# Feed-forward activations transposed by 32x32 blocks and transfers within SBUF in place of TensorE

## The chip, the cores and the metric

The kernel runs on one core of a Trainium2 chip. A core has five engines with instruction streams of their own: TensorE (PE in the profile, its weight loads PEld), VectorE (DVE), ScalarE (ACT), GpSimd (POOL) and SyncE (SP), which only issues transfers. Sixteen DMA engines carry the transfers. Working memory is SBUF with 128 partitions; matrix products land in PSUM. The metric is device time of one execution in microseconds.

## The reference

One layer of a diffusion backbone: modulated norm, a joint input projection, two kinds of attention, an output projection, and a SwiGLU feed-forward block. All is float32. What matters here is the last block, with 256 tokens, `D_MODEL` 2048 and `D_FF` 5632:

```python
def swiglu_sublayer(x, shift, scale, gate, norm_g, w_ff_gate, w_ff_up, w_ff_down):
    h = modulate(rms_norm(x, norm_g), shift, scale)
    return x + gate * ((jax.nn.silu(h @ w_ff_gate) * (h @ w_ff_up)) @ w_ff_down)
```

`gate` (called `a5` in the kernel) is one of six rows of `silu(c) @ w_ada + b_ada`.

## The kernel before

Every float32 operand of a product is split in two float32r parts, `hi` (rounded) and `lo` (the rest), and each product is three matmuls: hi x hi, hi x lo, lo x hi (`mm3`, lines 212 to 214).

`project` computes 256 tokens by 512 columns. It walks the contraction in steps of two 128-row tiles. For each step `load_w` brings 128x2x512 weights (512 KB) by one transfer on SP's queue into one of seven buffers `wraw` (line 200); ScalarE casts them to `whi` (L207), VectorE subtracts to `wlo` (L208), both in three buffers each; TensorE then does twelve matmuls of 512 columns, six for each of the two tiles of 128 tokens (`tk`).

The feed-forward block is a loop of eleven column groups `cg` of 512. In each, a gate product of eight steps ends in `g_evac` (ScalarE's Silu into `act`, L941) and an up product of eight steps ends in `u_evac` (VectorE multiplies, L944). The result `act[tk]` holds tokens on partitions and columns along the free dimension; the down product needs columns on partitions. So `turn` lets TensorE transpose four 128x128 pieces into PSUM (`ftp`, L951), and `split` writes `hi` and `lo` of the transposed tile `fT` (ScalarE L217, VectorE L218). `after(n, f)` puts `f` off by `n` steps, counting from the step in which it is called, so that the engines have other work meanwhile: `turn` runs in the first and second step of the next product. The down product (four groups of 22 steps, weights `w_ff_down`) comes behind the loop.

From `cg` 2 on, two more loads of 512 KB stand behind each product: pieces of `w_ada` (`wada`, line 388), which take `wraw` buffers too, and which VectorE adds up into `a5` (L395).

The framework's scheduler sets the order of each engine's instructions when the program is built, and puts in the semaphore waits. Each engine takes its own instructions strictly in order. Transfers issued by SP use eight semaphores in turn (DMAHW0 to DMAHW7), and each transfer waits until the last one of its own semaphore has landed: at most eight of SP's transfers are in flight. A weight load waits besides for the subtraction that frees its buffer.

Of the kernel before, what the change touches and what calls it, by code (L numbers as in the profile page):

```python
# [17 lines left out]
P = 128  # L18
# [27 lines left out]
def hybrid_block(ctx: ExitStack, tc: tile.TileContext, t: dict, out: bass.AP):  # L46
    nc = tc.nc
# [9 lines left out]
    def big_tile(name, dt=F32):  # L57
        return big.tile([P, 2048], dt, tag="big", name=name)
# [4 lines left out]
    def tp_ps(name="tp"):  # L63
        return psum.tile([P, CG], F32, tag="tp", bufs=2, name=name)
# [4 lines left out]
    def scratch(name, n=CG, dt=F32, tag="scr", bufs=3):  # L69
        return scr.tile([P, n], dt, tag=tag, bufs=bufs, name=name)  # L70
# [5 lines left out]
    ident = tab.tile([P, P], F32, name="ident")  # L76
# [139 lines left out]
    def split(hi, lo, src):  # L216
        nc.scalar.copy(out=hi, in_=src)  # L217
        nc.vector.tensor_tensor(out=lo, in0=src, in1=hi.bitcast(F32), op=ALU.subtract)  # L218
# [165 lines left out]
    def ada_pieces(a, chunk):  # L384

        for kt, hf in [(kt, hf) for kt in range(NKT) for hf in range(2)]:
            wt = wp.tile([P, 1024], F32, tag="wraw", bufs=WRAW, name="wada2")
            nc.sync.dma_start(out=wt, in_=w_ada[kt * P:(kt + 1) * P, chunk * D + hf * 1024: chunk * D + (hf + 1) * 1024])
            dst = a[:, hf * 1024:(hf + 1) * 1024]
            yield None  # L390
            with tc.issue_after(last_lo[-1].ins):
                if kt == 0:
                    nc.vector.tensor_scalar(out=dst, in0=wt, scalar1=sc[:, 0, 0:1], scalar2=None, op0=ALU.mult)
                else:
                    nc.vector.scalar_tensor_tensor(out=dst, in0=wt, scalar=sc[:, 0, kt:kt + 1], in1=dst, op0=ALU.mult, op1=ALU.add)  # L395
# [94 lines left out]
    def take(gen, n):  # L490
        for _ in range(n):
            if next(gen, gen) is gen:
                return

    def drain(gen):
        for _ in gen:
            pass
# [9 lines left out]
    def after(n, fn):  # L507
        late.append([n, fn])
# [66 lines left out]
    def project(src, hl, nkt, c0, evac, kt0=0, side=None, head=1, tail=1, hook=None):  # L575


        ps = [mm_ps() for _ in range(2)]
        nt = nkt // WK
        order = [(i, tk) for i in range(nt) for tk in range(2)]  # L580
        order[:2 * head] = [(i, tk) for tk in range(2) for i in range(head)]
        order[-2 * tail:] = [(i, tk) for tk in range(2) for i in range(nt - tail, nt)]
        wt = {}
        for n, (i, tk) in enumerate(order):
            if i not in wt:
                wt[i] = load_w(src, i * WK * P, c0, in_big=WHI <= i < head or nt - tail <= i < nt - WHI)
            wh, wl = wt[i]
            for j in range(WK):
                k = i * WK + j
                ah, al = hl.at(kt0 + k, tk * P, P)  # L590
                mm3(ps[tk], ah, al, wh[:, j], wl[:, j], k == 0, k == nkt - 1)
            if i == nt - 1 and (tail > 1 or tk == 1):
                for x in ([tk] if tail > 1 else range(2)):
                    evac(x, ps[x])
            if hook:
                hook(i, tk)
            if n % 2:
                tick()
                if side:
                    side()  # L600
                yield None
# [24 lines left out]
    def q_evac(qT, br):  # L626
        def f(tk, ps):
            o = norm_rope(ps, br, "q", tk)

            def turn():  # L630
                tp = tp_ps("qtp")
                for h in range(4):
                    nc.tensor.transpose(out=tp[:, h * P:(h + 1) * P], in_=o[:, h * P:(h + 1) * P], identity=ident)
                src = tp.rearrange("p (h q) -> p h q", h=4)
                split(qT[:, 0, :, tk * P:(tk + 1) * P], qT[:, 1, :, tk * P:(tk + 1) * P], src)
            after(5 + tk, turn)
        return f
# [79 lines left out]
    def unit(br, u):  # L717
        return (u // 4, u % 4) if br == "a" else (u // 8, u // 2 % 4)
# [59 lines left out]
    for n, (br, u) in enumerate(units):  # L778
        q = (br, unit(br, u)[0])
# [33 lines left out]
    for cg in range(4):  # L813
# [19 lines left out]
        def gated(tk, ps):  # L833
            g = gs[tk]
            nc.vector.tensor_tensor(out=g, in0=ps, in1=g, op=ALU.mult)
            nc.vector.tensor_tensor(out=m[tk], in0=m[tk], in1=g, op=ALU.add)
            after(2 + tk, turn(tk))

        def turn(tk, cg=cg, m=m):
            def f():  # L840
                tp = tp_ps("mtp")
                for j in range(4):
                    nc.tensor.transpose(out=tp[:, j * P:(j + 1) * P], in_=m[tk][:, j * P:(j + 1) * P], identity=ident)
                hi, lo = mT.four(cg, tk * P, P)
                split(hi, lo, tp.rearrange("p (h q) -> p h q", h=4))
            return f
# [84 lines left out]
    w_g, w_u, w_d = t["w_ff_gate"][0], t["w_ff_up"][0], t["w_ff_down"][0]  # L931
    NFT = DFF // P
    fT = Parts("fT", NFT)
    for cg in range(DFF // CG):
        if cg == 2:
            a5 = big_tile("ada5")
            a5_gen = ada_pieces(a5, 5)
        act = [scratch(f"act{tk}") for tk in range(2)]

        def g_evac(tk, ps):  # L940
            nc.scalar.activation(out=act[tk], in_=ps, func=AF.Silu)  # L941

        def u_evac(tk, ps):
            nc.vector.tensor_tensor(out=act[tk], in0=ps, in1=act[tk], op=ALU.mult)  # L944
            after(2 + tk, turn(tk))

        def turn(tk, cg=cg, act=act):
            def f():
                tp = tp_ps("ftp")
                for j in range(4):  # L950
                    nc.tensor.transpose(out=tp[:, j * P:(j + 1) * P], in_=act[tk][:, j * P:(j + 1) * P], identity=ident)  # L951
                hi, lo = fT.four(cg, tk * P, P)
                split(hi, lo, tp.rearrange("p (h q) -> p h q", h=4))
            return f

        drain(project(w_g, hT, NKT, cg * CG, g_evac, **(dict(head=TURN2, hook=head_hook) if cg == 0 else {})))
        if cg > 1:
            take(a5_gen, 2)
        drain(project(w_u, hT, NKT, cg * CG, u_evac))
        if cg > 1:  # L960
            take(a5_gen, 2)
# [47 lines left out]
```

## Time and profile before

| what | us |
|---|---|
| timed runs (3), median (lowest, highest) | 1733.82 (1732.61, 1733.86) |
| span of the profiled execution | 1730.7 |
| TensorE busy in it | 1706.1 |
| VectorE / ScalarE / GpSimd busy | 1132.6 / 775.0 / 135.5 |
| first and last transpose of `ftp` | 1041.8 and 1491.2 |

The profiled execution's time from its first instruction to its last is the span; the profile gives no other time for that execution. The median of the timed runs is 3.1 us above it, for what lies around the span. In the profile a row of the timeline reads: start in us, duration, engine, line, operation, output <- input. A q behind an engine's name means its instruction queue: a row of SPq is the issue of a transfer, not the transfer. Times within the feed-forward block are given on the span's clock.

### The profile page before, as it was taken

How to read it: one execution, taken by the hardware profiler on the slowest of the kernel's cores; microseconds unless marked ns; L12 is line 12 of the kernel's file. 1: busy time of each engine (PE TensorE's matmuls, PEld its weight loads, DVE VectorE, ACT ScalarE, POOL GpSimd, SP SyncE). 2: the span in 40 equal slices, each digit the busy share in tenths (PEclk: the TensorE clock that was granted, in tenths of full speed). 3: DMA queues.
4: the chain of work that ended last, by engine and by line, in shares of the span. 5: the costliest groups of instructions: out<-in, count | busy, mean ns of one | idle time of the engine just before them, and what ended most of it. 6: DMA issues, size and time to landing. Idle time of an engine off the chain costs nothing.

```text
span 1730.7 us, 21827 instructions
## 1 busy us (share of the span) xinstructions
PE 1706.1 (99%) x8150; PEld 1378.5 (80%) x8150; DVE 1132.6 (65%) x1428; ACT 775.0 (45%) x1063; POOL 135.5 (8%) x204
## 2 busy tenths in 40 slices
PE   7999999999999999999999999999999999999998
PEld 5667778887787788888888788888888888888887
DVE  5754668888788879796665754555565665454554
ACT  5222223245656556667544444444444444333332
POOL 2100001001131120002110100000000000000000
PEclk9999999999999999999999999999999999999999
DMA  9877785687766676777796766677777777666662
GB/s 263 300 242 265 233 319 174 201 271 235 252 189 202 212 265 217 247 227 248 249 323 222 237 180 190 201 237 241 234 242 234 240 236 231 208 213 197 221 205 88
DMA packets 192010, 397.69 MB, mean 230 GB/s; under 512 B 13504, under 2 KB 25872, under 8 KB 191392
## 3 DMA queue, kind: packets, MB, share of 16 engines
q1 hardware_dynamic: 183952, 369.71, 66.2%
q0 software_dynamic: 7952, 26.58, 4.8%
q8 instruction: 64, 1.05, 0.2%
q14 instruction: 42, 0.34, 0.1%
HBM read 385.72 MB, written 10.52 MB: 229 GB/s over the span
## 4 chain that ended last, share of the span: by engine, by line
PE 88%; DVE 5%; issue 3%; DMA 1%; ACT 1%; POOL 1%; SPq 0%; DVEq 0%; ACTq 0%; POOLq 0%
PE mm L212 26%; PE mm L213 26%; PE mm L214 26%; PE ada L268 2%; DVE wlo L208 1%; PE ptp L687 1%; PE o L705 1%; DMA wraw<-in_w_in_dram 1%; PE ftp L951 1%; PE s L667 1%; ACT whi L207 1%; PE o L213 0%; PE o L214 0%; PE o L212 0%; PE s L212 0%
## 5 line engine op out<-in xcount | busy, mean ns | idle before, releaser
L208 DVE TENSOR_TENSOR wlo<-wraw,whi 128x1024 fp32r<-128x1024 f32 (+1 forms) x506 | 611.6, 1210 | 460.2 <-ACT whi L207 458.8
L207 ACT CAST whi<-wraw 128x1024 fp32r<-128x1024 f32 (+1 forms) x506 | 527.7, 1043 | 796.6 <-PE mm L214 682.0
L213 PE MATMUL mm<-wlo,hT 128*128 128x512 f32 x696 | 271.0, 389 | 2.0 <-DVE wlo L208 2.0
L212 PE MATMUL mm<-whi,hT 128*128 128x512 f32 x696 | 272.8, 392 | 0.0
L214 PE MATMUL mm<-whi,hT 128*128 128x512 f32 x696 | 271.3, 390 | 0.1
L212 PE MATMUL mm<-whi,xT 128*128 128x512 f32 x640 | 257.2, 404 | 0.6 <-ACT whi L207 0.6
L213 PE MATMUL mm<-wlo,xT 128*128 128x512 f32 x640 | 251.5, 393 | 0.9 <-DVE wlo L208 0.9
L214 PE MATMUL mm<-whi,xT 128*128 128x512 f32 x640 | 250.5, 392 | 0.0
L213 PEld LDWEIGHTS mm<-wlo,hT 128*128 128x128 f32 x696 | 130.7, 188 | 28.8 <-DVE wlo L208 2.4
L214 PEld LDWEIGHTS mm<-whi,hT 128*128 128x128 f32 x696 | 130.6, 188 | 27.9 <-DVE hT L218 0.5
L395 DVE SCALAR_TENSOR_TENSOR ada<-wada,sc,ada 128x1024 f32<-128x1024 f32 x120 | 152.0, 1277 | 0.0
L212 PEld LDWEIGHTS mm<-whi,hT 128*128 128x128 f32 x696 | 130.7, 188 | 26.3
L212 PEld LDWEIGHTS mm<-whi,xT 128*128 128x128 f32 x640 | 120.1, 188 | 37.3 <-issue 9.8
L213 PEld LDWEIGHTS mm<-wlo,xT 128*128 128x128 f32 x640 | 120.8, 189 | 25.1 <-DVE wlo L208 2.4
L214 PEld LDWEIGHTS mm<-whi,xT 128*128 128x128 f32 x640 | 120.3, 188 | 25.4
L212 PE MATMUL mm<-whi,fT 128*128 128x512 f32 x352 | 137.2, 390 | 0.0
L214 PE MATMUL mm<-whi,fT 128*128 128x512 f32 x352 | 137.0, 389 | 0.0
L213 PE MATMUL mm<-wlo,fT 128*128 128x512 f32 x352 | 136.9, 389 | 0.0
L212 PEld LDWEIGHTS mm<-whi,fT 128*128 128x128 f32 x352 | 66.1, 188 | 14.5 <-issue 0.8
L212 PE MATMUL mm<-whi,cT 128*128 128x512 f32 x192 | 75.5, 393 | 1.8 <-ACT cT L344 1.8
L214 PEld LDWEIGHTS mm<-whi,fT 128*128 128x128 f32 x352 | 66.1, 188 | 13.9
L213 PEld LDWEIGHTS mm<-wlo,fT 128*128 128x128 f32 x352 | 66.1, 188 | 13.4
(237 smaller groups left out, 2115.2 us busy)
## 6 DMA issues: line engine op xcount, KB each, us to landing
wada<-in_w_ada_dram SPq DMA_DIRECT2D x192, 512.0 KB, 4.6
wraw<-in_w_in_dram SPq DMA_DIRECT2D x154, 512.0 KB, 4.6
wraw<-in_w_ff_gate_dram SPq DMA_DIRECT2D x88, 512.0 KB, 4.5
wraw<-in_w_ff_up_dram SPq DMA_DIRECT2D x88, 512.0 KB, 3.8
wraw<-in_w_ff_down_dram SPq DMA_DIRECT2D x88, 512.0 KB, 4.8
wraw<-in_w_br_a_dram SPq DMA_DIRECT2D x32, 512.0 KB, 5.0
wraw<-in_w_out_dram SPq DMA_DIRECT2D x32, 512.0 KB, 5.1
wraw<-in_w_br_b_dram SPq DMA_DIRECT2D x16, 512.0 KB, 5.4
```

Source lines behind the costliest of these rows:

```text
L207: last_hi.append(nc.scalar.copy(out=hi[:, 0:nk], in_=raw[:, 0:nk]))
L208: last_lo.append(nc.vector.tensor_tensor(out=lo[:, 0:nk], in0=raw[:, 0:nk], in1=hi[:, 0:nk].bitcast(F32), op=ALU.subtract))
L212: nc.tensor.matmul(ps, lhsT=ah, rhs=wh, start=first, stop=False)
L213: nc.tensor.matmul(ps, lhsT=ah, rhs=wl, start=False, stop=False)
L214: return nc.tensor.matmul(ps, lhsT=al, rhs=wh, start=False, stop=last)
L268: last_pe[0] = nc.tensor.matmul(aps[32 * g:32 * g + 32, 0:ncol], lhsT=cst[:, k, :], rhs=rhs, start=(k < 4), stop=(k >= NKT - 4))
L395: nc.vector.scalar_tensor_tensor(out=dst, in0=wt, scalar=sc[:, 0, kt:kt + 1], in1=dst, op0=ALU.mult, op1=ALU.add)
L667: nc.tensor.matmul(sps[i], lhsT=qT[rows, x, hh, tk * P:(tk + 1) * P], rhs=kT["b", grp][y][rows, hh, :], start=(n == 0), stop=(n == 2))
L687: nc.tensor.transpose(out=tp[:, kt * P:(kt + 1) * P], in_=p[:, kt * P:(kt + 1) * P], identity=ident)
L705: nc.tensor.matmul(op[:, 0:BV], lhsT=pT[:, kt, :], rhs=vb[:, kt, hh * BV:(hh + 1) * BV], start=(kt == 0), stop=(kt == 3))
L951: nc.tensor.transpose(out=tp[:, j * P:(j + 1) * P], in_=act[tk][:, j * P:(j + 1) * P], identity=ident)
```

## The change

`turn` goes. In `u_evac` VectorE transposes the tile within 32x32 blocks by one instruction (`fpart`), and sixteen transfers on SP's queue move each block of 32 partitions to where the full transpose has it (`fturn`): each moves 32 partitions by four runs of 32 floats, 16 KB. Eight of a tile's transfers are put off by 8 + 2 `tk` steps, the other eight by 9 + 2 `tk`, the split by 12 + 2 `tk`. The split now reads SBUF, not PSUM. The names `fpart` and `fturn` use scratch buffers (tags `nr` and `sq`, two each) that nothing else uses in this block.

```diff
+    def turned(src, dst_hi, dst_lo, tk):
+        part = scratch("fpart", tag="nr", bufs=2)
+        nc.vector.transpose(out=part, in_=src)
+        whole = []
+        def move(part_rows):
+            if not whole:
+                whole.append(scratch("fturn", tag="sq", bufs=2))
+            sv = part.rearrange("p (k b j) -> p b k j", k=4, b=4)
+            dv = whole[0].rearrange("p (k a j) -> p a k j", k=4, a=4)
+            for a in part_rows:
+                for b in range(4):
+                    nc.sync.dma_start(out=dv[32 * b:32 * b + 32, a], in_=sv[32 * a:32 * a + 32, b])
+        after(8 + 2 * tk, lambda: move((0, 1)))
+        after(9 + 2 * tk, lambda: move((2, 3)))
+        after(12 + 2 * tk, lambda: split(dst_hi, dst_lo, whole[0].rearrange("p (k q) -> p k q", k=4)))
...
         def u_evac(tk, ps):
             nc.vector.tensor_tensor(out=act[tk], in0=ps, in1=act[tk], op=ALU.mult)
-            after(2 + tk, turn(tk))
-
-        def turn(tk, cg=cg, act=act):
-            def f():
-                tp = tp_ps("ftp")
-                for j in range(4):
-                    nc.tensor.transpose(out=tp[:, j * P:(j + 1) * P], in_=act[tk][:, j * P:(j + 1) * P], identity=ident)
-                hi, lo = fT.four(cg, tk * P, P)
-                split(hi, lo, tp.rearrange("p (h q) -> p h q", h=4))
-            return f
+            turned(act[tk], *fT.four(cg, tk * P, P), tk)
```

SP's queue from behind the up product of group 2 to behind that of group 3, before (numbers in the names of `wada` are the buffer's; xN counts equal rows in a row):

```order
L200 DMA wraw<-in_w_ff_gate_dram 128x2x512 x8
L388 DMA wada_10082<-in_w_ada_dram 128x1024
L388 DMA wada_10085<-in_w_ada_dram 128x1024
L200 DMA wraw<-in_w_ff_up_dram 128x2x512 x8
L388 DMA wada_10236<-in_w_ada_dram 128x1024
```

The same stretch of SP's queue after the change:

```order
L200 DMA wraw<-in_w_ff_gate_dram 128x2x512 x7
L947 DMA fturn<-fpart 32x4x32 x8
L200 DMA wraw<-in_w_ff_gate_dram 128x2x512
L947 DMA fturn<-fpart 32x4x32 x8
L388 DMA wada_10145<-in_w_ada_dram 128x1024
L388 DMA wada_10148<-in_w_ada_dram 128x1024
L200 DMA wraw<-in_w_ff_up_dram 128x2x512
L947 DMA fturn<-fpart 32x4x32 x8
L200 DMA wraw<-in_w_ff_up_dram 128x2x512
L947 DMA fturn<-fpart 32x4x32 x8
L200 DMA wraw<-in_w_ff_up_dram 128x2x512 x6
```

The 32 transfers of a group stand between the seventh gate load and the third up load of the next group; the first eight come one place ahead of the last gate load. Seven rows of them with the semaphores that each waits for, from the first on (the first also waits for the block transpose, on VectorE's semaphore):

```order
L947 DMA fturn<-fpart 32x4x32 [waits DMAHW5_49,DVE_49]
L947 DMA fturn<-fpart 32x4x32
L947 DMA fturn<-fpart 32x4x32 [waits DMAHW7_49]
L947 DMA fturn<-fpart 32x4x32 [waits DMAHW0_49]
L947 DMA fturn<-fpart 32x4x32 [waits DMAHW1_49]
L947 DMA fturn<-fpart 32x4x32 [waits DMAHW2_49]
L947 DMA fturn<-fpart 32x4x32 [waits DMAHW3_49]
```

Each transfer takes the next of the eight semaphores, as the weight loads do. ScalarE, from the first cast into that group's `fT` on, before:

```order
L217 CAST fT_9943<-ftp 128x4x128
L207 CAST whi<-wraw 128x1024
L217 CAST fT_9943<-ftp 128x4x128
L207 CAST whi<-wraw 128x1024 x5
L941 ACTIVATE act_9916<-mm 128x512
L941 ACTIVATE act_9917<-mm 128x512
```

and after (the two rows of `whi` shown are the casts of the first and the second up load):

```order
L217 CAST fT_9965<-fturn 128x4x128
L207 CAST whi<-wraw 128x1024
L960 ACTIVATE act_9977<-mm 128x512
L960 ACTIVATE act_9978<-mm 128x512
L207 CAST whi<-wraw 128x1024
L217 CAST fT_9965<-fturn 128x4x128
```

The casts of `fT` moved from the start of the gate product to behind it, the second between the casts of the second and the third up load; the gate evacuations moved ahead of the second up load's cast. On TensorE, the first matmuls of the third up load's step, before:

```order
L212 MATMUL mm_10087<-whi_10127,hT1_8911 128x512
L213 MATMUL mm_10087<-wlo_10128,hT1_8911 128x512
L214 MATMUL mm_10087<-whi_10127,hT1_8911 128x512
L212 MATMUL mm_10087<-whi_10127,hT1_8911 128x512
L213 MATMUL mm_10087<-wlo_10128,hT1_8911 128x512
```

and after:

```order
L212 MATMUL mm_10150<-whi_10207,hT1_8911 128x512
L212 MATMUL mm_10151<-whi_10207,hT1_8911 128x512
L213 MATMUL mm_10150<-wlo_10208,hT1_8911 128x512
L214 MATMUL mm_10150<-whi_10207,hT1_8911 128x512
L212 MATMUL mm_10150<-whi_10207,hT1_8911 128x512
```

The second tile's L212 moved ahead of the first tile's L213, the first matmul that reads `wlo`.

## The prediction

> **What bounds the kernel now.** I read the page first, then the chain of waits, then the feed-forward stage by windows.
>
> ```profile
> span 1730.7 us, 21827 instructions
> PE 1706.1 (99%) x8150; PEld 1378.5 (80%) x8150; DVE 1132.6 (65%) x1428; ACT 775.0 (45%) x1063; POOL 135.5 (8%) x204
> ...
> PE 88%; DVE 5%; issue 3%; DMA 1%; ACT 1%; POOL 1%; SPq 0%; DVEq 0%; ACTq 0%; POOLq 0%
> PE mm L212 26%; PE mm L213 26%; PE mm L214 26%; PE ada L268 2%; DVE wlo L208 1%; PE ptp L687 1%; PE o L705 1%; DMA wraw<-in_w_in_dram 1%; PE ftp L951 1%; PE s L667 1%; ACT whi L207 1%; PE o L213 0%; PE o L214 0%; PE o L212 0%; PE s L212 0%
> ```
>
> TensorE is the bound, and the transposes to be removed (L951) stand on the chain with 1%. Two windows of the gate/up stage:
>
> ```profile
> core 0: us, PE busy (x) PEld busy (x) DVE busy (x) ACT busy (x) POOL busy (x), PEclk, DMA share, GB/s
> 1180.00:1220.00 40.00, 40.00 (x179) 33.11 (x178) 24.48 (x22) 16.11 (x18) 0.00 (x0) 1.00 0.74 236
> 1340.00:1380.00 40.00, 40.00 (x182) 33.14 (x181) 24.39 (x23) 17.53 (x19) 0.00 (x0) 1.00 0.78 239
> ```
>
> TensorE never pauses there, at full clock, while VectorE has 15 of 40 us free and the DMA engines a quarter. So time taken from TensorE shortens the run, but only while weights keep arriving. The change spends exactly that: places in SP's queue.
>
> **What leaves TensorE.** The groups of the transposed tile, and the first transpose on the timeline:
>
> ```profile
> L951 PE MATMUL ftp<-ident,act x88: 270/272/273, 1041.8 to 1491.2; 128*128 128x128 f32 x88
> L217 ACT CAST fT<-ftp x22: 579/580/581, 1043.0 to 1492.0; 128x512 fp32r<-128x512 f32 x22
> L218 DVE TENSOR_TENSOR fT<-ftp,fT x22: 681/683/685, 1044.3 to 1493.3; 128x512 fp32r<-128x512 f32 x22
> ```
>
> ```profile
> 1130.31 0.39 PE L213 MATMUL mm<-wlo,hT 128*128 128x512 f32 x1
> 1130.54 0.39 PE L214 MATMUL mm<-whi,hT 128*128 128x512 f32 x1
> 1130.77 0.60 PE L951 MATMUL ftp<-ident,act 128*128 128x128 f32 x4
> 1131.12 0.47 PE L212 MATMUL mm<-whi,hT 128*128 128x512 f32 x1
> 1131.43 0.39 PE L213 MATMUL mm<-wlo,hT 128*128 128x512 f32 x1
> ```
>
> Durations overlap, so starts must be used. Product matmuls start 0.227 apart. The L213 at 1131.43 puts its predecessor's start at 1131.20; the four transposes began at 1130.77, so they cost 0.43 to 0.44 us. 22 tiles x 0.44 = **9.7 us** leave TensorE. [...]
>
> **What VectorE and ScalarE gain.** 22 block transposes of 128x512. The nearest rows are an operation of that shape and the evacuations around it:
>
> ```profile
> 1127.75 1.28 DVE L944 TENSOR_TENSOR act<-mm,act 128x512 f32<-128x512 f32 x2
> ...
> 1148.22 1.05 ACT L207 CAST whi<-wraw 128x1024 fp32r<-128x1024 f32 x1 [1.66 <-PE mm L214]
> 1150.94 0.60 ACT L941 ACTIVATE act<-mm 128x512 f32<-128x512 f32 x1 [0.76 <-PE mm L214]
> ...
> 1152.51 1.23 DVE L208 TENSOR_TENSOR wlo<-wraw,whi 128x1024 fp32r<-128x1024 f32 x1 [1.97 <-ACT whi L207]
> ```
>
> I take 0.64 us each (bounds 0.3 and 1.3: half and twice). A pair adds 1.3 us ahead of the next `wlo`; the three `whi`/`wlo` buffers put that one a step (2.7 us) ahead of its matmul, so it is hidden. Without that cover a pair would cost 1.3 us, 14 us over eleven. The transposed tile is not needed before the down product, some 20 us to 450 us later, so its own lateness costs nothing by itself; what it can delay is what stands behind its cast on ScalarE and its subtraction on VectorE. Those wait for the sixteenth landing of their tile. The two splits keep their shapes and only read SBUF: I cost them at nothing. The ScalarE order (gate evacuations now ahead of the second up cast) leaves that `wlo` about ready when needed: nothing, with no cover left.
>
> **What SP gains: the disputed cost.** 352 transfers of 16 KB join 20 loads per group. Before:
>
> ```profile
> 1127.86 0.37 SPq L200 DMA_DIRECT2D wraw<-in_w_ff_gate_dram  x1
> 1130.58 3.06 SPq L388 DMA_DIRECT2D wada<-in_w_ada_dram  x2
> 1136.49 14.43 SPq L200 DMA_DIRECT2D wraw<-in_w_ff_up_dram  x8
> ...
> 1139.68 8.20 SPq L200 DMA_DIRECT2D wraw<-in_w_ff_up_dram  x5
> ...
> 1142.40 0.37 SPq L200 DMA_DIRECT2D wraw<-in_w_ff_up_dram  x1
> ```
>
> Columns: start, duration, engine, line. These are the last gate load, two `wada`, and the first three up loads, the place where the 32 transfers go. Prices of issue and of landing:
>
> ```profile
> 1.19 0.41 SPq L88 DMA_DIRECT2D cin<-in_c_ctx_dram  x1
> 1.65 0.41 SPq L99 DMA_DIRECT2D vec<-in_b_ada_dram  x1
> 2.11 0.42 SPq L100 DMA_DIRECT2D vec<-in_norm_g_dram  x1
> ...
> 14.77 5.07 SPq L96 DMA_DIRECT2D tok<-in_ctx_dram  x8
> ```
>
> ```profile
> L200 SPq DMA_DIRECT2D wraw<-in_w_ff_up_dram x88: 367/368/401, 989.6 to 1459.1; - x88
> ...
> L388 SPq DMA_DIRECT2D wada<-in_w_ada_dram x128: 328/340/642, 152.2 to 1422.8; - x128
> ...
> DMA to landing us min/median/max: 3.5/4.4/8.4
> ```
>
> ```profile
> GB/s 263 300 242 265 233 319 174 201 271 235 252 189 202 212 265 217 247 227 248 249 323 222 237 180 190 201 237 241 234 242 234 240 236 231 208 213 197 221 205 88
> ...
> wraw<-in_w_ff_gate_dram SPq DMA_DIRECT2D x88, 512.0 KB, 4.5
> wraw<-in_w_ff_up_dram SPq DMA_DIRECT2D x88, 512.0 KB, 3.8
> ...
> cin<-in_c_dram SPq DMA_DIRECT2D x1, 8.0 KB, 1.7
> ```
>
> Unhindered SP issues start 0.46 us apart; a load of three dimensions takes 0.04 longer than one of two (368 against 328), so a transfer of this kind gets **0.50 us** (0.46 at best). The eight `tok` loads take 0.64 us each though an issue lasts 0.33: each waits for the landing of the transfer eight places earlier, because SP has eight semaphores in turn. Lone landings lie between 3.5 and 4.5 us; I take **4.0**, near the 3.8 of the up loads. Loads that queue follow each other by 512 KB at 323 GB/s = 1.62 us. A small transfer lands in about 1.7 us, hidden by the eight places.
>
> By hand, on the clock of those rows. The products by the up matmul end at 1129.03, the first block transpose at 1129.7. SP, which wanted to issue the last gate load at 1127.86, stands at the first transfer until then. Eight transfers: gate load 1133.7, landed 1137.7. Eight more: the eighth goes at 1137.7. `wada` 1138.2 and 1138.7, first up load 1139.2; they land at 1142.2, 1143.8, 1145.4. Of the next eight the sixth, seventh and eighth wait for those three landings, so the second up load goes at 1145.9 (before: 1139.68) and lands at 1149.9; the last of the next eight waits for it, and the third up load goes at 1150.4 (before: 1142.40), landing at 1154.4. The second tile's sixteenth transfer, issued at 1149.9, lands about 1151.6; its cast of 0.58 us is done on ScalarE before that load arrives, so the new wait of ScalarE is hidden behind the load, as long as the load is late. Cast 1.05 and subtraction 1.22 with hand-overs: `wlo` ready at 1156.75.
>
> When is it needed? The gate product ended at 1150.94, so the up product began at 1150.78, now 0.88 earlier for two removed transposes; its third load comes after 24 matmuls of 0.227 = 5.44, at 1155.3, and two L212 now stand ahead of the first L213: 1155.8. **TensorE waits 1.0 us** in such a group. `wada` loads stand between gate and up loads in eight groups; the other three I cost at nothing, since without the two `wada` the walk's third load goes at least 1.0 us (two issues) and up to 4.2 us (two queued loads as well) sooner, which covers the 1.0; without that cover they would cost 3 us together. GpSimd's queue gets nothing new. After the third load SP has no transfer left until the next group, some 28 us later, and six loads at 1.62 us are caught up well before. Eight x 1.0 = 8.0.
>
> **Sum.** -9.7 + 8.0 = -1.7 us on a span of 1730.7, that is 1729.0; the timed median 1733.8 lies 3.1 above that span, so **1732 us**.
>
> **Rivals.** First, the cover holds. With 0.46 us an issue and 3.5 us a landing the same walk has the third up load issued at 1148.8, landed at 1152.3 and `wlo` ready at 1154.65, 1.1 before need: all of the 9.7 us stays, 1724. For it speaks the many lone landings below 4; against it that the transfers have one dimension more than the 0.46 rows.
>
> Second, slower, by the same eight places: with landings of 4.5, the gate loads' median, four landings in a row push the third up load to 1151.9, landed 1156.4, ready 1158.75: 2.95 us a group, 23.6 in eight, +13.9, 1748. It is slower from the wait that eats the gain, 1.2 us a group, a landing of 4.1. Against it: the gate median includes loads that queue.
>
> Third, small packets fill the DMA engines. Each transfer is 128 runs of 128 bytes, eight for each of 16 engines. Two mixes of packets, the whole span and its microseconds 20 to 60:
>
> ```profile
> q1 hardware_dynamic: 183952, 369.71, 66.2%
> ```
>
> ```profile
> q1 hardware_dynamic: 10367, 9.90, 78.2%
> ```
>
> The first gives 0.662 x 1730.7 x 16 / 183952 = 100 ns for 2010 bytes, the second 48 ns for 955. So 128 bytes cost between 6 (by bytes) and 48 ns; I take 20, as the two are nearly in proportion: 0.16 us a transfer, 5 us in a 44 us group, a share of 0.75 going to 0.87. From 45 ns (11.5 us) nothing is left; at 50 ns a group runs 1.8 us over beside the 1.0 above, 8 x 2.8 - 9.7 = +13, 1747. [...]
>
> **Chances.** Wait of 0.4 to 2.2 us a group, the forecast: 0.43 (own range 1727 to 1742). Cover holds: 0.27. Landings of 4.5: 0.18. Packets: 0.08. Something on VectorE or ScalarE: 0.04, counted as slower. What a measurement can tell from no change is 0.2%, 3.5 us: 1730.3 to 1737.3. The forecast's part below that is 0.10, inside 0.22, above 0.11. Faster 0.27 + 0.10 = 0.37; same 0.22; slower 0.11 + 0.18 + 0.08 + 0.04 = 0.41. The range runs from the cover that holds, 1723.5, to landings of 4.5 and full engines, 1750; 0.04 below and some 0.12 above are left out.
>
> **What the profile after would show.** Right: no L951, 22 block transposes near 0.6 us; gaps of about 1 us on TensorE before the third up load, released by ScalarE's cast or VectorE's `wlo`, those released by a load's landing; SP rows waiting for DMAs. Cover holds: no such gaps. Packets: DMA share near 1 and landings of all loads longer. The prediction is wrong if block transposes exceed 1.3 us, if landings fall below 3.5 or pass 4.5 beside the transfers, or if the issue interval is not 0.46 to 0.50.

## The result, and the profile after

| | us, median (lowest to highest) | ratio to before, 95% interval |
|---|---|---|
| before, same chip | 1733.84 (1732.61 to 1734.24) | |
| after | 1788.49 (1784.17 to 1793.64) | 1.0318 (1.0302 to 1.0335) |

The change made the kernel 3.2% slower; 1732 was forecast. The profiled execution of after is the longest of its four, 1793.64 us with a span of 1791.9. Head and chain of its page:

```profile
span 1791.9 us, 22208 instructions
PE 1724.5 (96%) x8062; PEld 1375.7 (77%) x8062; DVE 1145.7 (64%) x1450; ACT 776.7 (43%) x1063; POOL 134.7 (8%) x204
...
PE 70%; DMA 10%; DVE 8%; issue 4%; SPq 4%; ACT 3%; POOL 1%; ACTq 0%; DVEq 0%; POOLq 0%
PE mm L213 21%; PE mm L214 21%; PE mm L212 21%; DMA wraw<-in_w_ff_up_dram 6%; DVE wlo L208 4%; SPq L947 3%; DMA wraw<-in_w_in_dram 3%; ACT whi L207 3%; PE ada L268 1%; PE ptp L687 1%; PE o L705 1%; PE s L667 1%; PE o L213 0%; PE o L212 0%; PE o L214 0%
```

TensorE's share of the chain fell from 88% to 70%. In its place stand the up loads (`wraw<-in_w_ff_up_dram`, 6%), the steps behind them (`wlo`, `whi`) and the issue of the new transfers (SPq L947, 3%). The two windows shown of before, now of after, and two rows of its waits (total, times, longest):

```profile
1180.00:1220.00 40.00, 39.24 (x168) 31.82 (x168) 22.91 (x22) 14.16 (x15) 0.00 (x0) 0.98 0.65 207
1340.00:1380.00 40.00, 36.24 (x156) 28.63 (x155) 23.41 (x23) 16.02 (x17) 0.00 (x0) 1.00 0.64 199
```

```profile
ACT whi L207 <- DMA wraw<-in_w_ff_up_dram: 86.4, 48, 5.4
...
PEld mm L212 <- ACT whi L207: 37.0, 27, 2.7
```

TensorE now pauses, ScalarE waits 86 us for up loads, and the DMA engines are less busy than before (0.65 for 0.74): they are not what is full. Where the time went by stage, from the first matmul on `hT` (gate and up) and on `fT` (down); these rows are of before, then of after:

```profile
L212 PE MATMUL mm<-whi,hT x696: 388/389/477, 989.4 to 1483.0; 128*128 128x512 f32 x174
L212 PE MATMUL mm<-whi,fT x352: 389/389/499, 1484.8 to 1724.6; 128*128 128x512 f32 x176
```

```profile
L212 PE MATMUL mm<-whi,hT x696: 387/389/628, 997.8 to 1542.2; 128*128 128x512 f32 x174
L212 PE MATMUL mm<-whi,fT x352: 387/389/632, 1542.9 to 1785.9; 128*128 128x512 f32 x176
```

The gate/up stage grew from 1484.8 - 989.4 = 495.4 us to 545.1, what follows it from 245.9 to 249.0. The 8.4 us ahead of the stage belong to this execution: the instructions there stand in the same order in both kernels, and other kernels below began the stage between 989.8 and 994.2. Now SP's queue in the group whose block transpose starts at 1247.3:

```profile
1248.06 5.11 SPq L947 DMA_DIRECT2D fturn<-fpart  x8
1253.27 0.54 SPq L200 DMA_DIRECT2D wraw<-in_w_ff_gate_dram  x1
1253.85 5.09 SPq L947 DMA_DIRECT2D fturn<-fpart  x8
1259.04 1.01 SPq L388 DMA_DIRECT2D wada<-in_w_ada_dram  x2
1260.14 0.39 SPq L200 DMA_DIRECT2D wraw<-in_w_ff_up_dram  x1
1260.58 6.07 SPq L947 DMA_DIRECT2D fturn<-fpart  x8
1266.75 0.54 SPq L200 DMA_DIRECT2D wraw<-in_w_ff_up_dram  x1
1267.33 5.09 SPq L947 DMA_DIRECT2D fturn<-fpart  x8
1272.52 3.14 SPq L200 DMA_DIRECT2D wraw<-in_w_ff_up_dram  x6
```

Eight transfers take 5.1 us: SP is issuing without a pause, 0.645 us from one to the next. Only the third eight hold a wait for a landing (6.07). The second up load goes at +19.5 us behind the block transpose, the third at +25.2. What TensorE does then:

```profile
1270.91 0.39 PE L214 MATMUL mm<-whi,hT 128*128 128x512 f32 x1
1272.01 0.73 PE L212 MATMUL mm<-whi,hT 128*128 128x512 f32 x2 [0.71 <-ACT whi L207]
1273.27 0.50 PE L213 MATMUL mm<-wlo,hT 128*128 128x512 f32 x1 [0.53 <-DVE wlo L208]
...
1275.44 0.39 PE L214 MATMUL mm<-whi,hT 128*128 128x512 f32 x1
1277.43 0.73 PE L212 MATMUL mm<-whi,hT 128*128 128x512 f32 x2 [1.60 <-ACT whi L207]
1278.69 0.50 PE L213 MATMUL mm<-wlo,hT 128*128 128x512 f32 x1 [0.53 <-DVE wlo L208]
```

Each late load stops TensorE twice, for `whi` and then for `wlo`. Without a wait starts are 0.227 us apart, as in before (twice that behind a row with x2). By that the four stops cost 0.87 + 0.81 + 1.76 + 0.81 us, and four single starts around them, 0.32 to 0.34 apart, another 0.4: 4.7 us in this group. On the mean of ten groups, block transpose to block transpose, a group lasts 49.54 us, 6.0 more than the 43.52 of the kernels below in which TensorE does not stop.

Part of that is the granted clock (PEclk, the third number from the end). In seven of the ten groups, though not in the one above, it stood at 0.50 for 3.4 us right behind the stops for the third up load, and matmuls started 0.43 us apart in place of 0.227:

```profile
1229.40:1232.60 3.20, 3.20 (x9) 2.47 (x8) 1.92 (x2) 0.80 (x1) 0.00 (x0) 0.50 1.06 392
```

```profile
1230.30 0.63 PE L214 MATMUL mm<-whi,hT 128*128 128x512 f32 x1
1230.73 0.63 PE L213 MATMUL mm<-wlo,hT 128*128 128x512 f32 x1
```

Some 48 matmuls at 0.2 us more each make 9.6 of the 60 us that the ten groups lost. The same stretch of before, and of no_move, half_unread, three_quarters, spread and pool_tied below, has no such matmuls. What brings the lower clock on was not tried; in these groups it came only behind stops of TensorE.

### The profile page after: what moved, and what is told of

It is laid out like the page before. It is cut to its first block, busy times and chain, and to the rows that moved or that the text cites. A ratio compares the mean times of both kernels' runs of the same rounds, so it can differ in the third digit from the quotient of the medians.

```text
span 1791.9 us, 22208 instructions
## 1 busy us (share of the span) xinstructions
PE 1724.5 (96%) x8062; PEld 1375.7 (77%) x8062; DVE 1145.7 (64%) x1450; ACT 776.7 (43%) x1063; POOL 134.7 (8%) x204
## 3 DMA queue, kind: packets, MB, share of 16 engines
q0 software_dynamic: 7952, 26.58, 4.7%
## 4 chain that ended last, share of the span: by engine, by line
PE 70%; DMA 10%; DVE 8%; issue 4%; SPq 4%; ACT 3%; POOL 1%; ACTq 0%; DVEq 0%; POOLq 0%
PE mm L213 21%; PE mm L214 21%; PE mm L212 21%; DMA wraw<-in_w_ff_up_dram 6%; DVE wlo L208 4%; SPq L947 3%; DMA wraw<-in_w_in_dram 3%; ACT whi L207 3%; PE ada L268 1%; PE ptp L687 1%; PE o L705 1%; PE s L667 1%; PE o L213 0%; PE o L212 0%; PE o L214 0%
## 5 line engine op out<-in xcount | busy, mean ns | idle before, releaser
L212 PE MATMUL mm<-whi,hT 128*128 128x512 f32 x696 | 274.1, 398 | 21.5 <-ACT whi L207 21.5
L213 PE MATMUL mm<-wlo,hT 128*128 128x512 f32 x696 | 279.3, 401 | 14.9 <-DVE wlo L208 14.9
L214 PE MATMUL mm<-whi,hT 128*128 128x512 f32 x696 | 276.3, 397 | 0.1
L212 PE MATMUL mm<-whi,xT 128*128 128x512 f32 x640 | 257.9, 406 | 2.5 <-ACT whi L207 2.1
L213 PE MATMUL mm<-wlo,xT 128*128 128x512 f32 x640 | 252.7, 395 | 1.9 <-DVE wlo L208 1.8
L212 PEld LDWEIGHTS mm<-whi,hT 128*128 128x128 f32 x696 | 131.5, 191 | 57.0 <-ACT whi L207 30.3
L213 PEld LDWEIGHTS mm<-wlo,hT 128*128 128x128 f32 x696 | 133.6, 192 | 53.6 <-DVE wlo L208 26.0
L214 PEld LDWEIGHTS mm<-whi,hT 128*128 128x128 f32 x696 | 133.8, 192 | 28.1 <-DVE hT L218 0.5
L212 PEld LDWEIGHTS mm<-whi,xT 128*128 128x128 f32 x640 | 120.5, 189 | 39.8 <-issue 11.2
L213 PEld LDWEIGHTS mm<-wlo,xT 128*128 128x128 f32 x640 | 121.1, 189 | 26.8 <-DVE wlo L208 4.1
L212 PE MATMUL mm<-whi,fT 128*128 128x512 f32 x352 | 137.8, 391 | 1.4 <-ACT whi L207 1.4
L213 PE MATMUL mm<-wlo,fT 128*128 128x512 f32 x352 | 137.7, 391 | 0.8 <-DVE wlo L208 0.8
L212 PEld LDWEIGHTS mm<-whi,fT 128*128 128x128 f32 x352 | 66.4, 189 | 15.7 <-ACT whi L207 1.8
L213 PEld LDWEIGHTS mm<-wlo,fT 128*128 128x128 f32 x352 | 66.5, 189 | 14.8 <-DVE wlo L208 1.1
L212 PE MATMUL mm<-whi,cT 128*128 128x512 f32 x192 | 75.4, 393 | 1.7 <-ACT cT L344 1.7
```

Source lines behind the costliest of these rows:

```text
L212: nc.tensor.matmul(ps, lhsT=ah, rhs=wh, start=first, stop=False)
L213: nc.tensor.matmul(ps, lhsT=ah, rhs=wl, start=False, stop=False)
L214: return nc.tensor.matmul(ps, lhsT=al, rhs=wh, start=False, stop=last)
```

## The experiments

Theory A: the issues of the transfers hold up SP, so weight loads go out late. Rival B: the transfers fill the DMA engines. Rival C: the new order on ScalarE and VectorE, or a wait there for a transfer, makes `whi` and `wlo` late. "Group" is the mean of ten periods from block transpose to block transpose, "third load" the mean time from a group's block transpose to the issue of the third up load, over the seven groups in the middle that have `wada` loads in the same places. These two are of the profiled execution, the time is the median.

| kernel | transfers ahead of the third load | third load, us | group, us | time, us |
|---|---|---|---|---|
| no_move | 0 | 12.5 | 43.52 | 1724.06 |
| half_unread | 16 | 14.6 | 43.52 | 1722.70 |
| three_quarters | 24 | 20.7 | 43.88 | 1726.02 |
| spread_early | 28 | 23.8 | 47.67 | 1767.89 |
| long_runs | 32 | 24.8 | 48.00 | 1773.26 |
| unread | 32 | 25.7 | 48.99 | 1783.52 |
| after | 32 | 25.7 | 49.54 | 1788.49 |

**no_move** leaves out the transfers:

```diff
-        after(8 + 2 * tk, lambda: move((0, 1)))
-        after(9 + 2 * tk, lambda: move((2, 3)))
-        after(12 + 2 * tk, lambda: split(dst_hi, dst_lo, whole[0]...))
+        after(12 + 2 * tk, lambda: split(dst_hi, dst_lo, part...))
```

> The block transposes stay, the 352 transfers are left out, and the split reads fpart, which holds each 32x32 block transposed but not moved: the output is not the reference's. Theory A (the transfers take SP 0.645 us each, 20.6 us a group, and hold back the up loads behind them): all the loss goes and the 88 TensorE transposes stay saved, 1733.8 - 9.7 = 1724 us, no gaps of TensorE before the second and third up load. Rival B (the transfers slow the loads in the DMA engines): also about 1724. Rival C (the new place of the splits on ScalarE and VectorE, or the block transposes on VectorE, makes whi and wlo late): still about 1785 us with the same gaps.

1724.06 us, ratio 0.9931 (0.9916 to 0.9946), no gaps, every group 43.52. The whole loss hangs on the transfers, and the block transposes are hidden; C in its first form falls. Against before, where a group (from evacuation to evacuation of the up product) lasts 44.46, 0.94 us a group is saved. B is not told apart yet.

**unread** keeps all 352 transfers, but the split reads `part` as in no_move, so nobody waits for them.

> All 352 transfers run, but the split reads fpart and nobody waits for fturn (the output is not the reference's). Theory A: SP is as busy as before, so the gaps and the time stay: 1780 to 1792 us. Rival C (ScalarE's cast of fT waits for the sixteenth transfer and holds up the casts of the weights queued behind it): the gaps go, 1724 to 1735 us.

1783.52 us, 1.028 (1.0253 to 1.0306); a wait of ScalarE for `fturn` is not the cause. The intervals of the two times just touch. In the profiled executions its groups are 0.55 us shorter than those of after, 5.5 us in ten; but after's profile is of its longest execution, 5.2 us above its median, so that wait is worth half a microsecond a group or less.

```profile
ACT whi L207 <- DMA wraw<-in_w_ff_up_dram: 124.7, 51, 6.3
```

**pool_queue** issues the same transfers from GpSimd:

```diff
-                    nc.sync.dma_start(out=dv[32 * b:32 * b + 32, a], in_=sv[32 * a:32 * a + 32, b])
+                    nc.gpsimd.dma_start(out=dv[32 * b:32 * b + 32, a], in_=sv[32 * a:32 * a + 32, b])
```

> The same 352 transfers with the same runs of 128 bytes, issued by GpSimd's queue in place of SP's. Theory A: SP is free for the loads, 1724 to 1732 us, no gaps before the up loads. Rival B (45056 packets of 128 bytes in the DMA engines delay the loads): 1775 to 1790 us, since the packets are the same. If GpSimd needs more than 1.4 us for an issue, its 32 in a 44.9 us group end late and ScalarE's cast of fT holds up the weights behind it: above 1740 us.

1756.25 us, 1.011 (1.008 to 1.014): more than half of the loss is gone, and the time lies outside both theories' numbers. An issue takes GpSimd 0.55 us, not the 1.4 feared, but the transfers land later (3.6 us on the median, 1.9 from SP), and ScalarE is held:

```profile
L947 POOL DMA_DIRECT2D fturn<-fpart x352: 548/548/941, 1041.9 to 1522.9; - x176
```

```profile
1245.95 0.62 ACT L217 CAST fT<-fturn 128x512 fp32r<-128x512 f32 x1 [7.11 <-DMA fturn<-fpart]
1246.47 1.08 ACT L960 ACTIVATE act<-mm 128x512 f32<-128x512 f32 x2
1247.44 2.94 ACT L207 CAST whi<-wraw 128x1024 fp32r<-128x1024 f32 x3
```

ScalarE stood 7.1 us at the cast of `fT` with three weight casts queued behind it. Here C's second form is real.

**long_runs** writes `act` in block order, so that a transfer moves 32 partitions by one run of 512 bytes:

```diff
-            nc.vector.tensor_tensor(out=act[tk], in0=ps, in1=act[tk], op=ALU.mult)
+            nc.vector.tensor_tensor(out=by_block(act[tk]), in0=in_order(ps), in1=by_block(act[tk]), op=ALU.mult)
...
-            sv = part.rearrange("p (k b j) -> p b k j", k=4, b=4)
-            dv = whole[0].rearrange("p (k a j) -> p a k j", k=4, a=4)
+            sv = part.rearrange("p (b q) -> p b q", b=4)
+            dv = whole[0].rearrange("p (a q) -> p a q", a=4)
```

> Silu and the product write act in the order (b k j), so that each transfer moves 32 partitions by one run of 512 bytes in place of four of 128; there are as many transfers, with as many bytes. If an issue on SP costs by the runs (theory A1), it falls from 0.60 towards the 0.37 to 0.41 of the other loads and the interval to 0.46: 32 x 0.46 = 14.7 us a group, the third up load about 6 us earlier, 1724 to 1732 us. If an issue costs the same whatever the runs (A2: a price of a transfer from SBUF to SBUF): 0.60 us stays and the time too, 1780 to 1790 us.

1773.26 us, 1.0214 (1.0199 to 1.0229). An issue took 0.588 us in the middle, 0.633 from start to start: 11 ns less than with four runs. So A2, not A1: a quarter of the packets and nearly the old price, though the time lies below A2's range too. The 15 us gained are more than 32 x 0.011 = 0.35 us a group; the third load goes 0.9 us earlier and a group is 1.5 us shorter. Some 6 of the 15 are the clock: its profile has three of the slow stretches in ten groups, with 19 matmuls 0.43 us apart in place of 48 (granted clock over the whole execution 0.993 for 0.989). The rest is not settled.

**spread** puts four transfers behind each weight load over eight steps, and the splits later:

```diff
-        after(8 + 2 * tk, lambda: move((0, 1)))
-        after(9 + 2 * tk, lambda: move((2, 3)))
-        after(12 + 2 * tk, ...split...)
+        for n in range(4):
+            after(8 + n + 4 * tk, lambda n=n: move(pairs[4 * n:4 * n + 4]))
+        after(15 + 3 * tk, ...split...)
```

> The same 352 transfers on SP's queue, with the same runs, but put off so that four stand behind each weight load over eight steps (8 to 15), not eight behind each of four; the splits come 3 and 4 steps later. A load and four transfers take SP 0.41 + 4 x 0.645 = 3.0 us, a step of TensorE 2.73, so SP falls back by some 2 us in eight steps, less than the 7 us by which the loads are ahead. If the bunching on SP's queue is the cause (theory A): no gaps, 1724 us (to 1730). If 20.6 us of issues in a group are too many wherever they stand: 1760 to 1785 us.

1737.09 us, 1.002 (1.0009 to 1.0031), with all 352 transfers on SP, though 1724 was expected. No load is late any more (16 transfers ahead of the third load, which goes at 17.2). What is left is one stop in most groups, 1.3 us on the mean of ten. TensorE, then VectorE around it:

```profile
1216.63 0.61 PE L212 MATMUL mm<-whi,hT 128*128 128x512 f32 x2
1218.71 0.50 PE L213 MATMUL mm<-wlo,hT 128*128 128x512 f32 x1 [1.46 <-DVE wlo L208]
```

```profile
1215.48 0.69 DVE L963 TENSOR_TENSOR act<-mm,act 128x512 f32<-128x512 f32 x1 [2.10 <-PE mm L214]
1216.20 0.71 DVE L937 STREAM_TRANSPOSE fpart<-act 128x512 f32<-128x512 f32 x1
1216.84 0.69 DVE L963 TENSOR_TENSOR act<-mm,act 128x512 f32<-128x512 f32 x1
1217.44 1.22 DVE L208 TENSOR_TENSOR wlo<-wraw,whi 128x1024 fp32r<-128x1024 f32 x1
```

The scheduler had slipped the subtraction for the next gate step behind the evacuations of the up product, and VectorE stood idle 2.1 us ahead of them.

**pool_late** is pool_queue with the splits called 17 + `tk` steps behind.

> The transfers on GpSimd's queue as in pool_queue, and the two splits of a group put off by 5 and 4 steps more (17 and 18 in place of 12 and 14), so that ScalarE reaches the casts of fT some 11 us later. If what was left of the loss in pool_queue (a wait of up to 8 us of ScalarE for the last transfer, ahead of weight casts) is that wait: 1724 to 1730 us. If it is the transfers in the DMA engines (rival B): still 1745 to 1757 us.

1755.95 us, 1.0123 (1.0094 to 1.0151), and it tells nothing: the scheduler sorted the casts back, at +13 to +17 and +23 to +27 us behind the block transpose (the last group apart), as in pool_queue. A larger number in `after` did not move them.

**half_unread** is unread without the second eight transfers of each tile.

> Half of the transfers (eight of each tile) on SP's queue in the old places, and the split reads fpart, so the output is not the reference's. Theory A: 16 x 0.645 = 10.3 us a group in two bunches of 5.2 with loads between; the third up load is issued some 10 us earlier than in the kernel after the change, no gaps are left: 1724 to 1730 us. If the loss goes in proportion to the transfers: half of it, 1754 us.

1722.70 us, 0.9939 (0.9924 to 0.9954), no gaps. Not half of the loss but none of it: there is a threshold.

**issue_probe** adds six idle transfers a group to the kernel before, of eleven kinds:

> The kernel before with six idle transfers more in each of the eleven groups, of another kind in each (source SBUF or DRAM, 16, 32, 64 or 128 partitions, runs of 128 to 1024 bytes), to read how long SP takes to issue one. If the price hangs on the source (P1): 0.60 us for every kind that reads SBUF, 0.33 to 0.41 for those that read DRAM. If on the number of partitions (P2): 0.60 for those of 32 partitions from SBUF and from DRAM, 0.35 for those of 128.

```profile
L954 SPq DMA_DIRECT2D pdst<-psrc x42: 464/582/1407, 1041.6 to 1489.8; - x42
L954 SPq DMA_DIRECT2D pdst<-in_w_ff_gate_dram x18: 420/432/1620, 1226.8 to 1254.4; - x18
```

```profile
L954 SPq DMA_DIRECT2D probe_d<-psrc x6: 345/420/429, 1397.2 to 1402.3; - x6
```

`psrc` and `pdst` are in SBUF, `probe_d` and the weights in DRAM. Neither P1 nor P2: 0.42 us where only the source is in SBUF, 0.43 where only the destination is (32x4x32, 32x128 and 128x32 alike), 0.58 where both are, from 16 partitions of 1024 bytes to 128 of 128.

**spread_early** starts four steps of four transfers a tile at step 5, with the splits 12 + 3 `tk` steps behind.

> As spread (four transfers behind a weight load, on SP's queue, all 352), but from step 5 on and with the splits 12 and 15 steps behind, so that on VectorE the subtraction for the first gate step stays ahead of the up product's evacuation, which it had slipped behind in spread (a wait of 1.46 us in each of seven groups for wlo). Theory: SP's 20.6 us a group cost nothing once no load is late and VectorE's order is kept: groups of 43.5 us as without transfers, 1722 to 1728 us. If TensorE loses time to the transfers themselves: 1737 us as in spread, or more.

1767.89 us, 1.0193 (1.0179 to 1.0207): missed by 40 us. VectorE's order is mended, but three steps earlier means twelve transfers in a row ahead of the seventh gate load and 28 ahead of the third up load, which goes at 23.8:

```profile
1230.53 7.68 SPq L946 DMA_DIRECT2D fturn<-fpart  x12
1238.31 0.54 SPq L200 DMA_DIRECT2D wraw<-in_w_ff_gate_dram  x1
```

The largest stop already stands at the first up load, which goes at 16.5 behind 20 transfers (in after at 13.2 behind 16), so the third load's column does not tell all of this kernel's loss:

```profile
1252.45 0.73 PE L212 MATMUL mm<-whi,hT 128*128 128x512 f32 x2 [1.63 <-ACT whi L207]
```

I had reckoned with the spacing and not with the count ahead of the loads that decide. A version on SP with both put right was not tried.

**pool_tied** takes pool_queue and ties the split behind weight work of its step:

```diff
+            with tc.issue_after(last_hi[-1].ins):
+                nc.scalar.copy(out=dst_hi, in_=whole[0]...)
+            with tc.issue_after(last_lo[-1].ins):
+                nc.vector.tensor_tensor(out=dst_lo, in0=whole[0]..., in1=dst_hi..., op=ALU.subtract)
...
-        after(12 + 2 * tk, ...split...)
+        after(11 + 3 * tk, out_split)
```

> The transfers on GpSimd's queue, and the split tied behind the weight cast and the subtraction of the step in which it is called (12th and 15th), since the put-off of pool_late had left ScalarE's casts of fT in nearly the same place of its order (+14 and +24 us behind the block transpose). They now come some 8 us later, behind the last landing (+23 to +26 us). If the wait of ScalarE for those landings was the rest of the loss: 1722 to 1730 us. If packets in the DMA engines: 1745 us or more.

1723.96 us, 0.9946 (0.9932 to 0.996): faster than before by 0.5%, and the same work as in after on every engine but SP and GpSimd. Every group lasts 43.52 us. One window of 50 us and the second cast of `fT` in a group:

```profile
1200.00:1250.00 50.00, 50.00 (x223) 41.39 (x221) 30.44 (x29) 22.05 (x23) 17.40 (x32) 1.00 0.78 243
```

```profile
1242.21 0.62 ACT L953 CAST fT<-fturn 128x512 fp32r<-128x512 f32 x1 [0.26 <-DMA fturn<-fpart]
```

The DMA engines have a share of 0.78, and TensorE does not stop. With SP's queue free of the transfers and no reader held up, the whole loss is gone: that is theory A. Rival B needs another run, because the packets are not the same. Of the rows of the queues (packets, MB, share), the first is of after, the second of spread, the third of pool_tied; before has 183952 packets on q1 and 7952 on q0:

```profile
q1 hardware_dynamic: 234640, 375.50, 64.2%
q1 hardware_dynamic: 234640, 375.50, 67.1%
q0 software_dynamic: 19216, 32.37, 6.3%
```

The transfers add 5.79 MB either way, but 50688 packets from SP and 11264 from GpSimd. It is spread that rules B out: with the same packets as after on the same queue it took 1737.09 us, and not 1788.49.

**three_quarters** is unread with twelve transfers a tile:

> 24 of the 32 transfers of a group, in the old places; the split reads fpart (the output is not the reference's). 24 x 0.645 = 15.5 us on SP, about the 32 x 0.50 = 16.0 that the prediction reckoned with. If only the size of the issue interval was wrong in it and its walk was right: small waits of TensorE, 0 to 1.0 us a group, 1722 to 1733 us. If the walk was wrong as well (landings, places, casts): 1745 us or more.

1726.02 us, 0.9953 (0.9939 to 0.9966): within what the walk would have, and a point on the edge of the threshold.

**spread_early_long** is spread_early with the runs of long_runs.

> spread_early with runs of 512 bytes (Silu and the product write act in the order (b k j)): a quarter of the packets, the same number of issues. If spread_early is already free of waits, the same time as that, within 0.2%; faster only if packets cost anything.

1759.3 us, 1.0145 (1.0131 to 1.0158). spread_early was not free of waits, so its condition fell; as in long_runs, longer runs bring some 9 us, again with a third load that goes 0.8 us earlier. The clock explains nothing here (36 slow matmuls, 38 in spread_early; 0.993 and 0.992 over the whole execution); why the runs count stays open.

## Why the prediction was wrong

**The step that failed is the issue interval: "a transfer of this kind gets 0.50 us (0.46 at best)".** It measured 0.645 from start to start, 0.60 for the issue itself:

```profile
L947 SPq DMA_DIRECT2D fturn<-fpart x352: 585/599/1654, 1049.2 to 1565.6; - x176
```

I took the price from transfers between DRAM and SBUF and added for a dimension. The probe shows that shape and runs hardly matter and that both ends in SBUF do. 32 x 0.145 = 4.6 us a group. The third column is the prediction's own walk with 0.645 for each transfer and nothing else changed. Times count from the start of the block transposes, which the walk has at 1129.03:

| us | forecast | the same walk with 0.645 | after, group at 1247.3 | three_quarters, mean |
|---|---|---|---|---|
| SP on transfers ahead of the third load | 16.0 | 20.6 | 20.6 | 15.5 |
| second up load | 16.9 | 19.4 | 19.5 | 17.0 |
| third up load | 21.4 | 25.0 | 25.2 | 20.7 |
| TensorE lost, us a group | 1.0 | 4.6 | 4.7 | 0.5 |

With the measured price the walk meets this group, which ran at full clock, within 0.2 us. It then has the second load's `whi` late as well, by 0.8 us (0.87 in the trace), where the prediction expected a stop at the third load alone. Of SP's waits for landings little is left, as the issues fill that time: 1.2 us in the third eight by this walk, 1.0 in the trace (6.07 - 5.11), 2.2 in the forecast. three_quarters tests the walk from the other side: with SP's time near the one reckoned with, the third load goes 0.7 us sooner than forecast, and the seven groups in the middle last 44.03, 0.5 over 43.52. (Its bunches are of eight and of four, and nobody waits for its transfers.) So the walk (eight places, landings, the need at 1155.8) was right within a microsecond, and its price of an issue was wrong. The rows could not show it: nothing in the kernel before moves data within SBUF. But the bounds were too narrow. "0.46 at best" had no end on the other side but 0.50, taken from the nearest rows and widened only downwards, and the case that an interval beyond 0.50 brings stood in the last sentence without a price or a chance.

**The price is half of the miss.** Eight groups at 4.6 us and the saving of 9.7 give 1733.8 + 27.1 = 1761 us, not 1788. The other half are terms that the sum had at nothing:

- The groups without `wada`, which were to be covered by 1.0 to 4.2 us, lost time too. In after the first and the last of the ten periods last 48.73 and 47.74 us, 5.2 and 4.2 over 43.52, and behind the loop the last group's transfers, among the down loads, cost 4.0.
- The eight groups with `wada` lost 6.4 us on the mean in place of 4.6: 4.8 and 5.0 in the two at full clock, 4.9 to 7.6 in the six with a slow stretch. The walk had matmuls 0.227 us apart throughout; a slow stretch costs about 1.4 us. What else these groups lost is open.

**A steep threshold.** Up to a third load at 20.7 nothing much is lost; from there to 25.7 a group grows by 49.54 - 43.88 = 5.7 us for 5.0 us of delay, about one of it by the clock. At the edge of a cover a small error in a price that is paid 32 times weighs heavily.

**What was right.** The saving, 9.7 us for 0.44 a tile: no_move saves 11.2 by the medians, and 0.94 a group, 0.47 a tile. The mechanism, a third up load that waits behind transfers on SP, was right too. The block transposes, 0.684 us for 0.64, hidden:

```profile
L937 DVE STREAM_TRANSPOSE fpart<-act x22: 667/684/702, 1048.4 to 1544.4; 128x512 f32<-128x512 f32 x22
```

The small landing, 1.9 us for 1.7. Landings of 4.5, the slower rival, were not the reason: in four groups from 1247.3 on the second and third up loads landed in 3.7 to 4.1 us, and waits of SP for landings between its transfers come to some 12 us in the whole run. Packets were not either. In a window of 2 us in which hardly anything but transfers moved (last columns: DMA share, GB/s)

```profile
1249.30:1251.30 2.00, 2.00 (x11) 1.65 (x10) 1.30 (x2) 1.05 (x1) 0.00 (x0) 1.00 0.18 28
```

16 engines were busy 0.18 x 2 us for 56 KB, 437 packets of 128 bytes: 13 ns each, for the 20 taken. That is twice the 6 that the prediction reckoned by bytes, but at a share of 0.18 far from filling the engines.

**The loss by stage.** After against no_move: the gate/up stage 545.1 against 484.7 (its rows for no_move run from 993.0 to 1477.7), +60.4; what follows, 249.0 against 245.0, +4.0 from the last group's transfers among the down loads. Together 64.4. That the medians differ by 1788.49 - 1724.06 = 64.4 too is chance: the profiled executions differ by 1791.9 - 1722.7 = 69.2, with 4.8 of it ahead of the stage.

## What to carry to other kernels

An issuing queue is a resource with a price for each transfer, and a small transfer need not be cheap (here 0.60 us for 16 KB within SBUF, 0.37 for a load of 512 KB): multiply the price by the count that stands ahead of the next load that is needed, and compare it with how early that load goes now. Do so for each load behind the transfers, the first one too. If no row of the profile shows the kind of transfer, bound its price upwards too, and work out at which price the cover ends before choosing a value. Where another engine's queue is idle, put the small transfers there, and see where in the order the first reader of their data stands: here the queue alone was not enough (pool_queue), nor was a reader that waits for nothing (unread).

## What the runs showed of the hardware

- A transfer with both ends in SBUF takes SP 0.58 to 0.60 us to issue behind another of its kind (behind a load 0.46 to 0.57 in the probe, 0.59 to 0.74 in after), one with an end in DRAM 0.42 to 0.43 (medians of the probe). A weight load right behind such a transfer takes 0.54 us where one behind another load takes 0.39 (rows at 1253.27 and 1260.14). Why was not tried.
- The same transfers from GpSimd take 0.55 us an issue and land in 3.6 to 3.9 us, from SP in 1.9 in after and 1.8 to 3.0 in the other kernels (medians). The profile counts 16 packets of 1024 bytes for each from GpSimd, 128 of 128 bytes from SP. From SP an issue of 0.60 us stands against a landing of 1.9, and SP's queue without the transfers, once the splits had been tied, gave back 64 us (1788.49 to 1723.96). Whether nothing but SP's time was saved, these two runs can't tell, since the packets changed with the engine.
- Behind a stop, TensorE's next matmuls in after start 0.32 to 0.34 us apart in place of 0.227, so that a stop costs about 0.1 us beside itself.
- Between the first and the last block transpose the granted clock fell to 0.50 for 3.4 or 6.8 us at a time, with matmuls 0.43 us apart, in seven of the ten groups of after, in six of spread_early_long, in four of unread and of spread_early, in three of long_runs and of pool_late and in one of pool_queue. It did not in no_move, half_unread and pool_tied, which have no stops, nor in three_quarters and spread, whose stops for `wlo` are of 0.6 us at most and of 1.46 (the row at 1218.71). Over the whole profiled execution the granted clock was 0.989 in after, 0.990 in unread, 0.992 in spread_early and pool_late, 0.993 in spread_early_long and long_runs, 0.997 in pool_queue, and 0.998 or 0.999 in the five without.
